# Attention on one core: forget term, scaling and row extreme in one chained VectorE pass

## The chip, the cores and the metric

The kernel runs on one core of a Trainium2 chip. A core has five engines with a queue each: TensorE (PE; its weight loads are shown apart, as PEld), VectorE (DVE), ScalarE (ACT), GpSimd (POOL) and SyncE (SP, which issues DMAs). The metric is the device time of one execution in microseconds, and of several runs the median.

## The reference

One layer of a streaming encoder over 16 meta tokens and 1,024 frames: a norm, then forgetting attention beside a state-space model, merged by gates, an output projection, and a gated feed-forward with a short convolution. The change touches the softmax of the attention alone (8 heads of 64 columns, 1,040 positions):

```python
scale = 1.0 / math.sqrt(dh)          # 0.125
s = jnp.einsum('bqhd,bkhd->bhqk', qb, k, preferred_element_type=jnp.float32) * scale
s = s + jnp.transpose(fqb, (0, 2, 1))[..., None] - fk     # forget term: F[t] - F[s]
mask = k_pos[None, :] <= qp[:, None]
s = jnp.where(mask[None, None], s, -1e30)
p = jax.nn.softmax(s, axis=-1)
return jnp.einsum('bhqk,bkhd->bqhd', p.astype(v.dtype), v)
```

F[t] is the same for a whole row, so it falls out of the softmax.

## The kernel before

All matrix products keep a float32 operand as two parts (high and low) and add three products, lines L170 to L172. The attention goes over four pairs of heads (loop `pr`). In a pair, a unit is one head and one or two row tiles `c` of 128 query rows (the first tile has the 16 meta tokens); `KS[c]` is the number of keys up to the tile's end, `kc`, between 16 and 1,040. `scores` makes the softmax weights of one tile, `pv` multiplies those of a unit with the values, and units are staggered: the scores of a unit are written ahead of the value product of the unit before.

In `scores` (L796 to L833), the keys are cut into banks of up to 512 columns. For each, two matmuls (L817, L818) write raw scores into one of two PSUM buffers `sp`. VectorE then takes them out in pieces (L823): those left of the diagonal with the row of the forget term `fb` (-8 F[s], the same for all 128 partitions), the last one with `fm`, the diagonal block of `fb` with the upper triangle set to -1e30 by GpSimd (L807). Each pass adds the term, writes the sum to `pt` and leaves the maximum of its piece in a column of `mx`; in the profile it is a CUSTOM_DVE instruction and a READ_ACCUMULATOR, which writes the column (in the built order, ISA and ISA again). A tile has one to four pieces (`ns`). L828 takes the maximum of the columns (where there are several) and L829 multiplies it by -0.125. ScalarE computes Exp with that bias, scale 0.125, and the row's sum (L830); L831 inverts the sum on VectorE, and L832 scales the row on GpSimd. There are four `pt` buffers.

In `pv`, TensorE transposes blocks of `pt` into a PSUM buffer `tp` (L860, two buffers), ScalarE casts them to the high part `th` (L867), VectorE computes the low part `tl` (L868, recorded at the helper's line L137), and TensorE multiplies both with the values into `po` (L881, L882). L885 and L886 take the result out.

Beside this, `fill` strews other matmuls between those of the attention: the projection of the next pair's queries and keys and the gates (L170 to L172, three PSUM buffers `mm`). Their results go out through ScalarE (L600 to L610) and VectorE splits (L137).

The order of each engine's queue isn't the order of the code: a scheduler fixes it when the program is built, by its own estimate of what will be ready when. All engines then run their queues strictly in that order. So an edit in `scores` can move instructions of the whole attention.

Of the kernel before, what the change touches and what calls it, by code (L numbers as in the profile page):

```python
# [9 lines left out]
F = mybir.dt.float32  # L10
# [3 lines left out]
AF = mybir.ActivationFunctionType  # L14
ALU = mybir.AluOpType
AX = mybir.AxisListType
# [3 lines left out]
P = 128  # L20
# [38 lines left out]
def block_kernel(ctx, tc, x, meta, xbt, x0t, g1t, w_q, w_k, w_v, w_f, w_u, w_g, b_f, w_ao, lam_d, bw_d, cw_d,  # L59
                 d_sk, l_dt, w_glu, w_o, g2, w_up, cwt_d, w_dn, gf, out, dbg=None, upto=99):  # L60
    nc = tc.nc
    dbg = dbg or {}
    out = out[0]

    V, S, GP, PE, SY = nc.vector, nc.scalar, nc.gpsimd, nc.tensor, nc.sync

    def pool(stack, name, bufs=1, side=None, **k):
        return stack.enter_context(
            tc.tile_pool(name=name, bufs=bufs, side=side, reuse_waits="tile", **k))
# [9 lines left out]
    def mm_ps():  # L79
        mm_n[0] += 1  # L80
        if mm_n[1] and mm_n[0] % 4 == 0:
            return po_ps()
        return pp.tile([P, 512], F, tag="mm", name="mm", bufs=3)
# [4 lines left out]
    def s_ps(name="sp"):  # L88
        return pp.tile([P, 512], F, tag="sp", name=name, bufs=2)
# [304 lines left out]
    def u_product(b, m):  # L394
        ps = mm_ps()
        for k in range(KD):
            part(ps, m, k, *UBLK[b])
        return ps
# [28 lines left out]
    for m in range(4):  # L427
        ps = u_product(1, m)
        S.copy(us_part(1, m), by_chunks(ps[:, :UBLK[1][1]]))
    for b in (2, 3):  # L430
# [15 lines left out]
        for m in range(4):  # L446
            ps = u_product(b, m)
# [341 lines left out]
    ap = pool(st_a, "attn", side="left")  # L789
# [6 lines left out]
    def scores(t_, e, c, fb):  # L796
        t, n = TILES[c]
        kc = KS[c]
        Qs, Ks = t_[f"q{e}"], t_[f"k{e}"]
        hr = slice(64 * e, 64 * e + 64)  # L800
        m_ = max(n, 32)
        dg = kc - n

        qz = qzero[e][c % 2]
        GP.tensor_copy(qz[hr, :m_], Qs[hr, t:t + m_].bitcast(F))
        fm = ap.tile([P, P], F, tag="fm", name="fm", bufs=2)
        GP.affine_select(out=fm[:n, :n], in_=fb[:n, dg:kc], pattern=[[-1, n]],  # L807
                         compare_op=ALU.is_ge, fill=-1e30, base=0, channel_multiplier=1)
        pt = ap.tile([P, L], F, tag="pt", name="pt", bufs=4)
        mx = ap.tile([P, 4], F, tag="mx", name="mx", bufs=4)  # L810
        nb = -(-kc // 512)
        w = -(-kc // nb // 8) * 8
        ns = 0
        for b in range(nb):
            a0, a1 = b * w, min(kc, b * w + w)
            ps = s_ps()
            PE.matmul(ps[:m_, :a1 - a0], Qs[:, t:t + m_], Ks[:, a0:a1], start=True, stop=False)  # L817
            PE.matmul(ps[:m_, :a1 - a0], qz[:, :m_], t_["kl"][:, a0:a1], start=False, stop=True)  # L818
            for lo, hi, src in ((a0, min(a1, dg), fb), (max(a0, dg), a1, None)):
                if hi <= lo:  # L820
                    continue
                s_ = fb[:n, lo:hi] if src is not None else fm[:n, lo - dg:hi - dg]
                V.tensor_tensor_reduce(out=pt[:n, lo:hi], in0=ps[:n, lo - a0:hi - a0], in1=s_, scale=1.0,  # L823
                                       scalar=-3e38, op0=ALU.add, op1=ALU.max, accum_out=mx[:n, ns:ns + 1])
                ns += 1
        nm = ap.tile([P, 4], F, tag="nm", name="nm", bufs=4)
        if ns > 1:
            V.reduce_max(nm[:n, 0:1], mx[:n, :ns], axis=AX.X)  # L828
        V.tensor_scalar(nm[:n, 1:2], nm[:n, 0:1] if ns > 1 else mx[:n, :1], -0.125, None, ALU.mult)  # L829
        S.activation(pt[:n, :kc], pt[:n, :kc], AF.Exp, bias=nm[:n, 1:2], scale=0.125, accum_out=nm[:n, 2:3])  # L830
        V.reciprocal(nm[:n, 3:4], nm[:n, 2:3])  # L831
        GP.tensor_scalar(pt[:n, :kc], pt[:n, :kc], nm[:n, 3:4], 1.0, ALU.mult, ALU.mult)  # L832
        return pt  # L833

    def pv(h, cs, pts, ob):
# [93 lines left out]
    for pr in range(H // 2):  # L929
# [46 lines left out]
        for n_unit, (cs, e) in enumerate(units):  # L976
            if 0 < pr < 3 and n_unit and n_unit % 2 == 0:
                out_weight_sums(4 * (pr - 1) + n_unit // 2 - 1, marks[-1])
            pts = [scores(qk, e, c, fbs[e]) for c in cs]
            if prev:  # L980
                second(*prev)
            prev = (cs, e, pts)
# [86 lines left out]
    for i in range(KD):  # L1069
# [6 lines left out]
        for t, n in QBLK:  # L1076
            ps = mm_ps()
# [962 lines left out]
```

## Time and profile before

| | us |
|---|---|
| median of three runs | 1444.65 (1443.22 to 1447.25) |
| profiled execution, its own time | 1442.12 |
| its span, first to last instruction | 1440.2 |
| granted TensorE clock, share of full speed | 0.998 |

In the lines of the profile, a group is a line of the kernel, its engine and operation, the tiles it writes and reads (out<-in), shapes and count. A timeline's columns are the start (us), the busy time, engine, line, operation and shape; in brackets stands the engine's idle time ahead of it and what ended that. A wait is put as "who <- for whom: us in total, times, longest us".

### The profile page before, as it was taken

How to read it: one execution, taken by the hardware profiler on the slowest of the kernel's cores; microseconds unless marked ns; L12 is line 12 of the kernel's file. 1: busy time of each engine (PE TensorE's matmuls, PEld its weight loads, DVE VectorE, ACT ScalarE, POOL GpSimd, SP SyncE). 2: the span in 40 equal slices, each digit the busy share in tenths (PEclk: the TensorE clock that was granted, in tenths of full speed). 3: DMA queues.
4: the chain of work that ended last, by engine and by line, in shares of the span. 5: the costliest groups of instructions: out<-in, count | busy, mean ns of one | idle time of the engine just before them, and what ended most of it. 6: DMA issues, size and time to landing. Idle time of an engine off the chain costs nothing.

```text
span 1440.2 us, 26617 instructions
## 1 busy us (share of the span) xinstructions
PE 1422.0 (99%) x9655; PEld 1346.8 (94%) x9655; DVE 1069.2 (74%) x2201; ACT 722.9 (50%) x1421; POOL 766.2 (53%) x887
## 2 busy tenths in 40 slices
PE   8999999999999999999999999999999999999997
PEld 8999999988999999999879999999999999888886
DVE  7999788843657676656469987788787875798867
ACT  7646585423646565533646544444443445643443
POOL 1542258642466556515861335455655545788795
PEclk9999999999999999999999999999999999999999
DMA  8686644530147422167963255677744327964443
GB/s 304 169 182 164 152 104 149 151 107 30 38 125 167 125 71 67 45 220 245 265 150 134 72 140 161 165 180 192 185 132 114 95 78 255 329 213 132 127 93 117
DMA packets 92967, 214.05 MB, mean 149 GB/s; under 512 B 15090, under 2 KB 22898, under 8 KB 92452
## 3 DMA queue, kind: packets, MB, share of 16 engines
q1 hardware_dynamic: 74132, 168.15, 35.3%
q0 software_dynamic: 17696, 41.29, 15.1%
q10 hardware_dynamic: 1008, 2.91, 0.5%
q8 instruction: 76, 1.25, 0.4%
q14 instruction: 55, 0.45, 0.1%
HBM read 170.88 MB, written 71.71 MB: 168 GB/s over the span
## 4 chain that ended last, share of the span: by engine, by line
PE 94%; DMA 2%; issue 2%; DVE 1%; ACT 1%; POOL 1%; POOLq 0%; DVEq 0%; SPq 0%; ACTq 0%
PE mm L172 5%; PE mm L170 5%; PE mm L171 5%; PE sp L233 4%; PE sp L232 4%; PE sp L234 4%; PE mm L232 3%; PE mm L234 3%; PE tp L232 3%; PE mm L233 3%; PE tp L233 3%; PE tp L234 3%; PE tp L860 3%; PE mm L1563 2%; PE mm L1562 2%; PE mm L1561 2%
## 5 line engine op out<-in xcount | busy, mean ns | idle before, releaser
L170 PE MATMUL mm<-xhi,whi 128*128 128x342 f32 (+2 forms) x480 | 157.0, 327 | 1.2 <-DVE q L137 1.0
L172 PE MATMUL mm<-xhi,wlo 128*128 128x342 f32 (+2 forms) x480 | 155.5, 325 | 0.0
L171 PE MATMUL mm<-xlo,whi 128*128 128x342 f32 (+2 forms) x480 | 155.2, 324 | 0.0
L1183 POOL TENSOR_TENSOR ov<-ov,og 128x1024 f32<-128x1024 f32 x21 | 50.8, 2421 | 118.1 <-ACT og L1182 115.7
L137 DVE TENSOR_TENSOR sw<-sf,sw 128x512 fp32r<-128x512 f32 x72 | 72.6, 1008 | 44.8 <-ACT sw L1174 43.6
L1174 ACT CAST sw<-sf 128x512 fp32r<-128x512 f32 x72 | 44.9, 624 | 109.7 <-POOL sf L1321 84.4
L170 PEld LDWEIGHTS mm<-xhi,whi 128*128 128x128 f32 x480 | 90.6, 189 | 2.5 <-PE sp L818 0.8
L172 PEld LDWEIGHTS mm<-xhi,wlo 128*128 128x128 f32 x480 | 90.4, 188 | 0.6 <-issue 0.2
L171 PEld LDWEIGHTS mm<-xlo,whi 128*128 128x128 f32 x480 | 90.5, 189 | 0.2
L867 ACT CAST th<-tp 128x256 fp32r<-128x256 f32 (+3 forms) x120 | 56.1, 471 | 62.1 <-PE tp L860 29.8
L137 DVE TENSOR_TENSOR tl<-tp,th 128x256 fp32r<-128x256 f32 (+3 forms) x120 | 65.1, 546 | 25.6 <-ACT th L867 24.1
L1321 POOL TENSOR_TENSOR sf<-raw,sf 128x512 f32<-128x512 f32 x36 | 63.5, 1764 | 38.7 <-DVE sw L137 38.6
L1321 POOL TENSOR_TENSOR sf<-raw 128x512 f32<-128x512 f32 x36 | 48.6, 1351 | 61.3 <-DMA raw<-in_w_up_dram 38.9
L234 PE MATMUL mm<-xhi,sw 128*128 128x258 f32 (+1 forms) x288 | 81.1, 281 | 0.0
L232 PE MATMUL mm<-xhi,sw 128*128 128x258 f32 (+1 forms) x288 | 80.8, 281 | 0.0
L233 PE MATMUL mm<-xlo,sw 128*128 128x258 f32 (+1 forms) x288 | 80.8, 281 | 0.0
L832 POOL TENSOR_SCALAR pt<-pt,nm 128x144 f32<-128x144 f32 (+4 forms) x72 | 52.3, 739 | 49.6 <-DVE nm L831 48.8
L1373 DVE SCALAR_TENSOR_TENSOR ov<-hv,cwt,ov 128x1024 f32<-128x1024 f32 x36 | 68.4, 1900 | 0.4 <-ACT ov L1371 0.4
L1174 ACT CAST sw<-raw 128x512 fp32r<-128x512 f32 x70 | 43.0, 620 | 47.6 <-PE sp L234 23.9
L830 ACT ACTIVATE pt<-pt,nm 128x144 f32<-128x144 f32 (+4 forms) x72 | 52.9, 735 | 26.4 <-DVE nm L829 26.0
L823 DVE CUSTOM_DVE_ANT_0 pt<-sp,fb 128x328 f32<-128x328 f32 (+8 forms) x112 | 46.4, 430 | 20.0 <-PE sp L818 11.0
L137 DVE TENSOR_TENSOR sw<-raw,sw 128x512 fp32r<-128x512 f32 x70 | 57.2, 821 | 5.2 <-ACT sw L1174 4.9
(719 smaller groups left out, 5726.3 us busy)
## 6 DMA issues: line engine op xcount, KB each, us to landing
raw<-in_w_up_dram SPq DMA_DIRECT2D x44, 512.0 KB, 3.7
t_d<-in_w_dn_dram POOLq DMA_DIRECT2D x44, 256.0 KB, 7.1
wr<-t_d SPq DMA_DIRECT2D x44, 256.0 KB, 3.9
ar<-a_d SPq DMA_DIRECT2D x41, 256.0 KB, 5.2
a_d<-ov SPq DMA_DIRECT2D x18, 512.0 KB, 2.6
wr<-in_w_dn_dram SPq DMA_DIRECT2D x33, 256.0 KB, 4.0
t_d<-in_w_dn_dram SPq DMA_DIRECT2D x22, 256.0 KB, 4.5
t_d<-t_d SPq DMA_DIRECT2D x22, 256.0 KB, 4.8
```

Source lines behind the costliest of these rows:

```text
L137: return eng.tensor_tensor(out_, src, hi.bitcast(F), ALU.subtract)
L170: yield PE.matmul(ps, whi[:, i, :], ahi[:, i], start=(i == 0), stop=False)
L171: yield PE.matmul(ps, whi[:, i, :], alo[:, i], start=False, stop=False)
L172: yield PE.matmul(ps, wlo[:, i, :], ahi[:, i], start=False, stop=(i == k - 1))
L232: PE.matmul(ps, a[0][:, i], bh, start=(i == 0 and not joins), stop=False, skip_group_check=True)
L233: PE.matmul(ps, a[0][:, i], bl, start=False, stop=False, skip_group_check=True)
L234: PE.matmul(ps, a[1][:, i], bh, start=False, stop=(i == kh - 1), skip_group_check=True)
L830: S.activation(pt[:n, :kc], pt[:n, :kc], AF.Exp, bias=nm[:n, 1:2], scale=0.125, accum_out=nm[:n, 2:3])
L867: S.copy(th[:kn, z:tw], tp[:kn, z:tw])
L1174: S.copy(hi, src)
L1321: sums.append(GP.tensor_tensor(f_, a, b, op))
L1373: V.scalar_tensor_tensor(out=o, in0=h_[:, j:SEQ + j], scalar=cwc(j, m), in1=o, op0=ALU.mult, op1=ALU.add)
```

## The change

The scale goes into the pass (-0.125 there), so that it leaves negated scores in `pt`, and the extreme becomes a minimum, whose result is the bias of Exp as it stands. In place of a column for each piece that is reduced afterwards, each pass starts its minimum from the column of the pass before (`low`). L828 and L829 fall away, `nm` has two columns and not four, and Exp takes scale -1 and the last column of `mx` as bias.

```diff
+        low = 3e38
         ...
-                V.tensor_tensor_reduce(out=pt[:n, lo:hi], in0=ps[:n, lo - a0:hi - a0], in1=s_, scale=1.0,
-                                       scalar=-3e38, op0=ALU.add, op1=ALU.max, accum_out=mx[:n, ns:ns + 1])
+                V.tensor_tensor_reduce(out=pt[:n, lo:hi], in0=ps[:n, lo - a0:hi - a0], in1=s_, scale=-0.125,
+                                       scalar=low, op0=ALU.add, op1=ALU.min, accum_out=mx[:n, ns:ns + 1])
+                low = mx[:n, ns:ns + 1]
                 ns += 1
-        nm = ap.tile([P, 4], F, tag="nm", name="nm", bufs=4)
-        if ns > 1:
-            V.reduce_max(nm[:n, 0:1], mx[:n, :ns], axis=AX.X)
-        V.tensor_scalar(nm[:n, 1:2], nm[:n, 0:1] if ns > 1 else mx[:n, :1], -0.125, None, ALU.mult)
-        S.activation(pt[:n, :kc], pt[:n, :kc], AF.Exp, bias=nm[:n, 1:2], scale=0.125, accum_out=nm[:n, 2:3])
-        V.reciprocal(nm[:n, 3:4], nm[:n, 2:3])
-        GP.tensor_scalar(pt[:n, :kc], pt[:n, :kc], nm[:n, 3:4], 1.0, ALU.mult, ALU.mult)
+        nm = ap.tile([P, 2], F, tag="nm", name="nm", bufs=4)
+        S.activation(pt[:n, :kc], pt[:n, :kc], AF.Exp, bias=low, scale=-1.0, accum_out=nm[:n, 0:1])
+        V.reciprocal(nm[:n, 1:2], nm[:n, 0:1])
+        GP.tensor_scalar(pt[:n, :kc], pt[:n, :kc], nm[:n, 1:2], 1.0, ALU.mult, ALU.mult)
```

The built order is the same up to the attention and behind it. Within it, VectorE's queue changes most. In the first pair of heads, before, these rows stand on VectorE around the three passes over a tile with 784 keys (`pt_4646`, pieces of 392, 264 and 128):

```order
L823 ISA pt_4646,mx_4647<-sp_4648,fb_4181 128x392
L823 ISA mx_4647 128x1
L831 RECIPROCAL nm_4635<-nm_4635 128x1
L823 ISA pt_4646,mx_4647<-sp_4652,fb_4181 128x264
L823 ISA mx_4647 128x1
L823 ISA pt_4646,mx_4647<-sp_4652,fm_4642 128x128
L823 ISA mx_4647 128x1
L886 TENSOR_TENSOR ob_4537<-po_4538,ot_4616 64x256
L137 TENSOR_TENSOR tl_4677<-tp_4671,th_4676 128x512
L828 TENSOR_REDUCE nm_4657<-mx_4647 128x1
L829 TENSOR_SCALAR nm_4657<-nm_4657 128x1
```

Of the changed kernel, the next tile with such pieces in the same pair (`pt_4751`; lines behind L823 lie a line further down, or a line up behind L828):

```order
L824 ISA pt_4751,mx_4752<-sp_4753,fb_4183 128x392
L824 ISA mx_4752 128x1
L824 ISA pt_4731,mx_4732<-sp_4737,fm_4727,mx_4732 128x128
L824 ISA mx_4732 128x1
L830 RECIPROCAL nm_4742<-nm_4742 128x1
L885 TENSOR_TENSOR ob_4519<-po_4641,ot_4722 64x256
L137 TENSOR_TENSOR tl_4772<-tp_4768,th_4771 128x256
L824 ISA pt_4751,mx_4752<-sp_4757,fb_4183,mx_4752 128x264
L824 ISA mx_4752 128x1
L137 TENSOR_TENSOR tl_4781<-tp_4775,th_4780 128x512
L824 ISA pt_4751,mx_4752<-sp_4757,fm_4747,mx_4752 128x128
L824 ISA mx_4752 128x1
```

The second and third pass read `mx`, the result of the one before, which is the link; the scheduler puts work of other rows between the links, and the two small instructions are gone.

On TensorE, at the first place where a value product meets the next scores, 10 us into the attention, these stood before (`sp_4433` is the second bank of a tile of 528 keys, `po_4352` the first value product of a whole tile):

```order
L860 MATMUL tp_4360<-ident_66,pt_4271 128x128
L860 MATMUL tp_4360<-ident_66,pt_4289 128x128
L817 MATMUL sp_4433<-k0_2519,q0_2517 128x264
L818 MATMUL sp_4433<-kl_2521,qz00_4173 128x264
L881 MATMUL po_4352<-th_4356,vt_3888 128x256
L817 MATMUL sp_4504<-k1_2520,q1_2518 128x400
L818 MATMUL sp_4504<-kl_2521,qz11_4176 128x400
L170 MATMUL mm_4735<-xhi_97,whi_4569 128x384
```

and now:

```order
L859 MATMUL tp_4350<-ident_66,pt_4269 128x128
L859 MATMUL tp_4350<-ident_66,pt_4285 128x128
L880 MATMUL po_4342<-th_4346,vt_3888 128x256
L818 MATMUL sp_4421<-k0_2519,q0_2517 128x264
L819 MATMUL sp_4421<-kl_2521,qz00_4173 128x264
L818 MATMUL sp_4490<-k1_2520,q1_2518 128x400
L819 MATMUL sp_4490<-kl_2521,qz11_4176 128x400
L170 MATMUL mm_4713<-xhi_97,whi_4551 128x384
```

The first value product moved ahead of the score pair. On VectorE, the passes that fill and free the banks at this place stood like this (`sp_4411` and `sp_4429` are the two banks):

```order
L823 ISA pt_4409,mx_4410<-sp_4411,fb_4181 128x272
L823 ISA mx_4410 128x1
L823 ISA pt_4409,mx_4410<-sp_4411,fm_4405 128x128
L823 ISA mx_4410 128x1
L823 ISA pt_4427,mx_4428<-sp_4429,fb_4181 128x264
L823 ISA mx_4428 128x1
L137 TENSOR_TENSOR q0_4185<-mm_4470,q0_4185 64x384
L137 TENSOR_TENSOR q1_4186<-mm_4470,q1_4186 64x384
```

and now (`sp_4401` and `sp_4417`):

```order
L824 ISA pt_4399,mx_4400<-sp_4401,fb_4181 128x272
L824 ISA mx_4400 128x1
L824 ISA pt_4415,mx_4416<-sp_4417,fb_4181 128x264
L824 ISA mx_4416 128x1
L824 ISA pt_4399,mx_4400<-sp_4401,fm_4395,mx_4400 128x128
L824 ISA mx_4400 128x1
L137 TENSOR_TENSOR q0_4185<-mm_4456,q0_4185 64x384
L137 TENSOR_TENSOR q1_4186<-mm_4456,q1_4186 64x384
```

The diagonal pass of the first tile, now a linked one, stands behind the first pass of the second tile; the splits of q stand behind all three, as before.

## The prediction

> **What bounds the kernel now.** I read the first part of the page for shares, then the chain that ended last, then windows over the attention, because a share over the whole span hides stages.
>
> ```profile
> span 1440.2 us, 26617 instructions
> ...
> PE 1422.0 (99%) x9655; PEld 1346.8 (94%) x9655; DVE 1069.2 (74%) x2201; ACT 722.9 (50%) x1421; POOL 766.2 (53%) x887
> ...
> PE 94%; DMA 2%; issue 2%; DVE 1%; ACT 1%; POOL 1%; POOLq 0%; DVEq 0%; SPq 0%; ACTq 0%
> ```
>
> TensorE is busy for 1422.0 of 1440.2 us, and 94% of the chain that ended last is its own work; VectorE holds 1% of it. The edited lines (L823 to L831) run between 347 and 612 us, so the next view is the windows of that stretch (columns: length, then busy time of PE, weight load, DVE, ACT and POOL, granted clock, DMA share, GB/s), and who TensorE waited for in it:
>
> ```profile
> 347.00:390.00 43.00, 41.15 (x272) 38.99 (x271) 27.90 (x136) 26.28 (x68) 24.88 (x58) 1.00 0.11 32
> 390.00:460.00 70.00, 69.61 (x489) 67.92 (x488) 45.94 (x199) 39.07 (x96) 39.11 (x80) 1.00 0.50 137
> 460.00:530.00 70.00, 69.69 (x491) 68.15 (x490) 48.11 (x208) 42.38 (x103) 39.40 (x82) 1.00 0.40 99
> 530.00:612.00 82.00, 81.74 (x582) 80.26 (x580) 52.00 (x228) 46.48 (x109) 47.00 (x87) 1.00 0.19 62
> ```
> ```profile
> PE mm L170 <- DVE q L137: 1.0, 2, 0.5
> PE po L882 <- DVE tl L137: 0.9, 3, 0.3
> PE sp L817 <- DVE mx L823: 0.6, 1, 0.6
> ```
>
> TensorE's idle time is 1.85 + 0.39 + 0.31 + 0.26 = 2.8 us of 265, at a full clock. VectorE is busy for 27.90 + 45.94 + 48.11 + 52.00 = 174 us and so has 91 us free. Of TensorE's named waits only the last (0.6 us, once) is for an edited pass; the split of q queued behind such passes (1.0 us) is the other that the edit can touch.
>
> Busy time can flatter TensorE, as matmul ends are modelled. So I looked at starts, in a quiet and in a disturbed place:
>
> ```profile
> 473.12 0.60 PE L860 MATMUL tp<-ident,pt 128*128 128x128 f32 x4
> 473.47 0.41 PE L170 MATMUL mm<-xhi,whi 128*128 128x342 f32 x1
> 473.71 0.32 PE L171 MATMUL mm<-xlo,whi 128*128 128x342 f32 x1
> 473.87 0.32 PE L172 MATMUL mm<-xhi,wlo 128*128 128x342 f32 x1
> ```
> ```profile
> 419.39 0.38 PE L881 MATMUL po<-th,vt 128*128 128x256 f32 x1
> 420.11 0.38 PE L882 MATMUL po<-tl,vt 128*128 128x256 f32 x1 [0.34 <-DVE tl L137]
> 420.33 0.28 PE L881 MATMUL po<-th,vt 128*128 128x256 f32 x1
> 420.45 0.28 PE L882 MATMUL po<-tl,vt 128*128 128x256 f32 x1
> ```
>
> A 342-column matmul has a slot of 0.16 us until the next starts (473.71 to 473.87); right behind a run of transposes it is 0.24 us (473.47 to 473.71), 0.08 more. At 419.39 a slot that is 0.12 us in the last two rows took 0.72: 0.60 lost, of which the page calls 0.34 idle. So true waiting is up to about twice the idle time: an estimate of 5.6 us for the stage. That is the most that any cure of TensorE's waits here can bring, 0.4%. The Trainium skill, page "Trainium Kernel Development and Optimization", section "Performance Expectations", warns of just this: matmul busy time is a bad measure, and weight-load busy time a good one. The weight-load column above (67.92 of 70.00 us) leaves more room than the matmul column (69.61), 2.08 instead of 0.39 us, which by that rule is a bound on the gain of the same small size.
>
> **What goes.** A row tile's passes stand on VectorE; the small instructions behind them are these:
>
> ```profile
> L828 DVE TENSOR_REDUCE nm<-mx x64: 132/151/158, 350.9 to 609.1; 128x1 f32<-128x3 f32 x32, 128x1 f32<-128x2 f32 x24, 128x1 f32<-128x4 f32 x8
> L829 DVE TENSOR_SCALAR nm<-nm x64: 130/153/157, 351.1 to 609.2; 128x1 f32<-128x1 f32 x64
> L829 DVE TENSOR_SCALAR nm<-mx x8: 135/141/142, 348.1 to 549.0; 16x1 f32<-16x1 f32 x8
> L823 DVE CUSTOM_DVE_ANT_0 pt<-sp,fb x112: 168/436/633, 350.4 to 608.4; 128x264 f32<-128x264 f32 x16, 128x328 f32<-128x328 f32 x16, 128x352 f32<-128x352 f32 x16, 128x16 f32<-128x16 f32 x8
> L823 DVE CUSTOM_DVE_ANT_0 pt<-sp,fm x72: 151/285/292, 347.9 to 608.7; 128x128 f32<-128x128 f32 x64, 16x16 f32<-16x16 f32 x8
> ```
>
> Removed: 64 x 0.151 + 64 x 0.153 + 8 x 0.141 = 9.7 + 9.8 + 1.1 = **20.6 us of VectorE**. The 112 + 72 = 184 passes stay, in the same shapes; another scale, a minimum for a maximum, and Exp with scale -1 and its bias from another tile change no size, so I put them at nothing.
>
> **What comes.** 184 - 72 = 112 passes now read the running extreme of the pass before as a [128, 1] operand, and so wait for its accumulator read. Such a wait is shown at the reduction:
>
> ```profile
> 382.52 0.43 DVE L823 CUSTOM_DVE_ANT_0 pt<-sp,fb 128x264 f32<-128x264 f32 x1
> 382.87 0.08 DVE L823 DVE_READ_ACCUMULATOR2_ANT mx<- 128x1 f32 x1
> 382.87 0.29 DVE L823 CUSTOM_DVE_ANT_0 pt<-sp,fm 128x128 f32<-128x128 f32 x1
> 383.08 0.08 DVE L823 DVE_READ_ACCUMULATOR2_ANT mx<- 128x1 f32 x1
> 383.20 0.15 DVE L828 TENSOR_REDUCE nm<-mx 128x1 f32<-128x3 f32 x1
> 383.39 0.15 DVE L829 TENSOR_SCALAR nm<-nm 128x1 f32<-128x1 f32 x1
> ```
> ```profile
> 383.57 0.95 ACT L830 ACTIVATE pt<-pt,nm 128x784 f32<-128x784 f32 x1 [1.92 <-DVE nm L829]
> ```
>
> A pass that needs nothing of the one before starts together with the accumulator read (382.87 and 382.87); the reduction, which needs it, starts 0.12 us after that read's start (383.08 to 383.20). I price a link at 0.12 us. In the built order 42 of the 112 links stand directly behind their own accumulator read, 42 x 0.12 = 5.0 us; between the ends of the other 70 stands at least one other VectorE instruction, and those cost VectorE nothing (0.12 us each, 8.4 us more, if that cover were gone). The Trainium skill, page "VectorE: DVE Perf Modes", section "The DRAIN you can't avoid", has it that a semaphore between two VectorE instructions costs nothing extra, since the next one waits for the pipeline anyway. The rows above disagree, 0.12 us against 0.00; by that page the 5.0 us would be 0. The per-partition operand itself has no row: its price lies between nothing and a whole small instruction, 0.15 us (L829), or 16.8 us for 112. Below nothing it cannot lie, since the pass goes over the same elements. I take nothing, the nearest rows being L828 and L829, which differ in what they read and not by 0.01 us in what they take. VectorE thus changes by -20.6 + 5.0 = -15.6 us; the bounds are -20.6 and +9.6 (8.4 and 16.8 us more). Either end is small beside its 91 us free, so neither moves the end by itself.
>
> **The chain of one row.** From the start of the last accumulator read to Exp it takes 383.57 - 383.08 = 0.49 us now, and without the two small steps 0.12: 0.37 less. A row of 2, 3 or 4 pieces gives back 0.12, 0.24 or 0.36 in links where nothing stands between. So Exp is ready 0.25 us earlier for 24 rows, 0.13 for 32, and no earlier for 8. Behind it stand Exp, the reciprocal, GpSimd's scaling and only then the transposes, for which TensorE has no wait worth naming in the list above. What is late next is the bank or the split, not the row.
>
> **TensorE's place in it.** Here is the one wait for a pass, and the split behind it:
>
> ```profile
> 357.67 0.60 PE L860 MATMUL tp<-ident,pt 128*128 128x128 f32 x4
> 358.91 0.39 PE L817 MATMUL sp<-k,q 128*128 128x264 f32 x1 [0.65 <-DVE mx L823]
> ...
> 360.51 0.41 PE L170 MATMUL mm<-xhi,whi 128*128 128x384 f32 x1 [0.48 <-DVE q L137]
> ```
> ```profile
> 358.20 0.44 DVE L823 CUSTOM_DVE_ANT_0 pt<-sp,fb 128x272 f32<-128x272 f32 x1 [1.51 <-PE tp L860]
> ...
> 359.24 1.12 DVE L137 TENSOR_TENSOR q<-mm,q 64x384 fp32r<-64x384 f32 x2
> ```
>
> The transposes free a pt buffer, three passes follow, then the two splits until 360.36, and L170 starts at 360.51. In the new order (shown with the change) TensorE puts the value product ahead of the two score pairs here, and VectorE puts the 264-column pass ahead of the diagonal one, so the bank of the first comes free some 0.35 us later (the slot of such a pass, 382.52 to 382.87). TensorE then waits for ScalarE's cast of the transposes instead of the bank, but the same three passes and two splits still end near 360.4, and L170 cannot start before. I cost this place at 0. The transposes of 128 columns stand in 113 runs before and 116 now: 3 x 0.08 = **+0.25 us**. The 0.37 us that a row's end gains may spare one of the short split waits: **-0.3 us**, an estimate, for the three named po waits lie at 0.3 at most. The other engines' moves (GpSimd's masks and scalings by a place or two, SyncE two pairs of loads and stores swapped) are covered by the 2.8 us bound: no transfer is named among TensorE's waits.
>
> **Sum.** +0.25 - 0.3 = -0.05, about 0. The profiled execution took 1442.1 us (1440.2 us of span and 1.9 around it), so 1442.1 again; it lies 2.5 below the median of the runs, 1444.65. Forecast for a median: **1444.5 us**.
>
> **Rivals.**
> - *VectorE sets the pace of the attention after all.* For it: the three waits named are all for VectorE. Against: its 91 us free. The Trainium skill, page "VectorE: DVE Perf Modes", section "Rules for kernel authors", says of chained VectorE operations to minimize their count and not the semaphores, and would so count this change as a gain. The time if all waiting went: 1444.65 - 5.6 = 1439 us. Chance 7%.
> - *The links hold PSUM banks.* A bank of scores is free only when all its pieces are read; a diagonal piece that waits, or stands behind another row's pass, frees it later, and TensorE's next L817 waits in the place of the reduction. It decides wherever TensorE asks for the bank again within that delay. If each of the 64 rows with links stalls TensorE for one link, 64 x 0.12 = 7.7 us, 1452 us. For it: 358.91 is such a wait. Against: it happens once in the stage, for 0.6 us. Chance 6%.
> - *It doesn't do what it says:* the pass with the [128, 1] operand is so slow that VectorE becomes the bound. To use up 91 + 20.6 us, 112 passes would have to cost 1.0 us more each, over twice the 0.436 us of one; the stage then grows from zero at that point, 1455 us with 0.1 us beyond it. Chance 2%.
> - Forecast: 85%.
>
> **Numbers.** A measurement of this kernel can tell about 0.3% from no change, 4.3 us: below 1440.3 is faster, above 1449.0 slower. The forecast's own range is 1444.5 with 2.8 us of idle time either way. The repeated runs spread from 1443.2 to 1447.3, so a median can lie a further 1.5 us off: 1440.2 to 1448.8. The first rival gives faster (7%), the second and third slower (8%), and the forecast spills 1% over each edge: faster 8%, same 83%, slower 9%. The range is 1440.2 to 1448.8, which leaves out the rivals, 15%.
>
> **What would show it.** Right: no L828 or L829 on VectorE, 184 passes of the old durations, a chained pass 0.12 us behind its accumulator read, VectorE's busy time down by 15 to 21 us, and TensorE busy for the same 262 us of the attention. Wrong: waits of L817 for L823's bank in number (second rival), passes over 0.6 us at the old shapes (third), or TensorE's slots behind 419.39 and the like at 0.12 us (first).

## The result: 0.16% slower, and where 2 us went

The changed kernel took 1446.8 us (median of 22 runs, 1442.5 to 1452.6), the kernel before beside it 1444.4 (22 runs): a ratio of 1.0016, interval 1.0009 to 1.0023. That is 2.3 us (1.3 to 3.3) more. It lies inside the 0.3% that the prediction called no change, but the interval leaves 1 out: the sum of about zero was wrong by 2 us. The profiled execution took 1447.3 us. Lines L817 to L825 now stand one lower; from Exp on (L829 now) they stand one higher.

The page of the changed kernel, its first lines and the chain that ended last:

```profile
span 1445.4 us, 26567 instructions
...
PE 1422.4 (98%) x9655; PEld 1345.5 (93%) x9655; DVE 1072.3 (74%) x2065; ACT 721.4 (50%) x1421; POOL 762.1 (53%) x887
...
PE 88%; DMA 3%; issue 3%; DVE 2%; ACT 2%; POOL 1%; SPq 0%; POOLq 0%; DVEq 0%; ACTq 0%
```

TensorE does the same work, but holds 88% of the chain, where it held 94%; transfers and three engines have moved in. The windows (columns as before) say where: the second of the four shown before, and one from 347 to 626 us that holds the end of the attention in both kernels, first of the changed kernel, then of the kernel before:

```profile
390.00:460.00 70.00, 68.53 (x475) 66.04 (x474) 42.67 (x159) 38.32 (x95) 39.43 (x81) 1.00 0.51 137
...
347.00:626.00 279.00, 274.15 (x1903) 266.04 (x1902) 174.24 (x640) 157.93 (x385) 152.38 (x311) 1.00 0.31 85
```
```profile
347.00:626.00 279.00, 275.50 (x1917) 268.01 (x1916) 179.72 (x776) 159.49 (x386) 152.35 (x311) 1.00 0.32 88
```

TensorE is busy for 68.53 of the 70 us, where it was 69.61: most of the loss lies between 390 and 460 us. VectorE's busy time in the attention fell from 179.72 to 174.24 us, by 5.5, not by 15.6. (Its total on the page even rose, from 1069.2 to 1072.3 us; one split behind the attention alone took 5.0 us more, see the last section.) TensorE's named waits in the attention, of the changed kernel:

```profile
PE po L880 <- ACT th L866: 1.5, 3, 1.0
PE po L881 <- DVE tl L137: 0.9, 3, 0.3
PE mm L170 <- DVE q L137: 0.8, 2, 0.5
PE po L880 <- DVE ob L885: 0.8, 1, 0.8
```

The wait for a pass is gone, as forecast. New is the last line, a value product that waits for the addition into `ob`, 0.8 us at once; of the 1.5 us for a cast, 1.0 is the place at 358 us whose change of waits was foreseen.

To measure the attention by itself I take a **stage**, from the start of the first score matmul to the start of the last value product on TensorE. Those are the first and the last start in these two groups, of the kernel before and then of the changed one:

```profile
L817 PE MATMUL sp<-k,q x120: 172/323/457, 291.4 to 607.6; 128*128 128x264 f32 x16, 128*128 128x328 f32 x16, 128*128 128x392 f32 x16, 128*128 128x456 f32 x16
...
L882 PE MATMUL po<-tl,vt x200: 251/282/389, 353.4 to 621.8; 128*128 128x256 f32 x96, 16*128 16x16 f32 x4
```
```profile
L818 PE MATMUL sp<-k,q x120: 170/323/457, 291.6 to 610.0; 128*128 128x264 f32 x16, 128*128 128x328 f32 x16, 128*128 128x392 f32 x16, 128*128 128x456 f32 x16
...
L881 PE MATMUL po<-tl,vt x200: 251/281/386, 353.3 to 624.1; 128*128 128x256 f32 x96, 16*128 16x16 f32 x4
```

With two decimals the stage took 621.76 - 291.43 = 330.33 us before and 624.07 - 291.62 = 332.45 after: **2.12 us** longer. TensorE runs the same number of instructions up to any point, so the n-th starts can be set side by side. From 217 us to the attention the two traces agree to 0.02 us; then two steps appear, **place A** (0.05 to 0.92 between 406 and 414 us) and **place B** (0.86 to 1.82 between 441 and 449 us); the rest of the stage adds up to 0.3.

Behind the stage, both profiles of the changed kernel lose another 2.8 us, 0.7 near 970 us and 2.1 near 1304, in code that the change does not touch. With the stage that would be 4.9 us, and the median is 2.3 longer, 3.3 at most: so not every execution can lose all of it. How many do is open. What follows is about the stage.

**Place A.** GpSimd, SyncE, ScalarE and TensorE of the changed kernel, and then of the kernel before:

```profile
400.41 2.40 POOL L137 TENSOR_TENSOR wlo<-raw,whi 128x1024 fp32r<-128x1024 f32 x1
402.78 1.07 POOL L508 TENSOR_SCALAR gs<-gs 128x1026 f32<-128x1026 f32 x1
402.84 0.33 SPq L148 DMA_DIRECT2D raw<-in_w_g_dram  x1
403.88 0.32 SPq L512 DMA_DIRECT2D g_d<-gs  x1
410.67 0.46 ACT L499 ACTIVATE gs<-mm 128x342 f32<-128x342 f32 x1 [5.63 <-DMA g_d<-gs]
...
411.10 0.32 PE L170 MATMUL mm<-xhi,whi 128*128 128x342 f32 x1
411.65 0.39 PE L880 MATMUL po<-th,vt 128*128 128x256 f32 x1 [0.23 <-ACT th L866]
```
```profile
400.61 1.08 POOL L508 TENSOR_SCALAR gs<-gs 128x1026 f32<-128x1026 f32 x1
...
401.71 0.32 SPq L512 DMA_DIRECT2D g_d<-gs  x1
...
406.47 0.46 ACT L499 ACTIVATE gs<-mm 128x342 f32<-128x342 f32 x1 [1.49 <-DMA g_d<-gs]
```

The scheduler put GpSimd's scaling of a finished gate behind a weight split of 2.40 us. The store of that gate, `g_d`, goes out 2.2 us later, and on SyncE behind a load of 512 KB. `gs` has one buffer, so ScalarE's next gate step waits for the store, now 5.63 instead of 1.49 us, and everything queued behind that step on ScalarE waits too: the cast `th`, for which TensorE leaves a slot of 0.55 us at 411.10 where it takes 0.16.

**Place B.** The same view some 40 us on, of the changed kernel and then of the kernel before:

```profile
439.78 0.74 ACT L829 ACTIVATE pt<-pt,mx 128x528 f32<-128x528 f32 x1 [0.73 <-DVE mx L824]
...
441.10 0.37 ACT L884 COPY ot<-po 64x256 f32<-64x256 f32 x1
...
442.34 0.33 SPq L963 DMA_DIRECT2D o_d<-ob  x1
...
449.07 0.30 PE L859 MATMUL tp<-ident,pt 128*128 128x128 f32 x1
...
449.70 0.42 DVE L885 TENSOR_TENSOR ob<-po,ot 64x256 f32<-64x256 f32 x1 [0.78 <-DMA o_d<-ob]
...
450.17 0.39 PE L880 MATMUL po<-th,vt 128*128 128x256 f32 x1 [0.80 <-DVE ob L885]
```
```profile
438.78 0.37 ACT L885 COPY ot<-po 64x256 f32<-64x256 f32 x1
439.31 0.74 ACT L830 ACTIVATE pt<-pt,nm 128x528 f32<-128x528 f32 x1 [0.16 <-DVE nm L829]
...
440.35 0.33 SPq L964 DMA_DIRECT2D o_d<-ob  x1
...
446.83 0.42 DVE L886 TENSOR_TENSOR ob<-po,ot 64x256 f32<-64x256 f32 x1 [0.55 <-DMA o_d<-ob]
...
447.97 0.28 PE L881 MATMUL po<-th,vt 128*128 128x256 f32 x1
```

Before, ScalarE took the finished value sums out (`ot`) ahead of the Exp of 528 columns; now the Exp stands ahead of the copy, and has to wait for its chained passes. The addition into `ob` and the store of `ob` start later, and this store is slow, because GpSimd's queue is loading `w_o`: the transfers issued from 434 to 443 us in the changed kernel (issues, KB each, median us to landing):

```profile
to_d<-in_w_o_dram POOLq DMA_DIRECT2D x2, 1024.0 KB, 10.6
o_d<-ob SPq DMA_DIRECT2D x1, 128.0 KB, 7.3
```

`ob` has one buffer and `po` one bank, so the next addition waits for the landing, and TensorE for the addition. Before, the addition was done at 447.25, 0.7 us ahead of TensorE's turn at 447.97. The Trainium skill, page "DMA: Bandwidth & Descriptors", section "Issuing engines are not separate DMA queues", says that transfers that ScalarE, SyncE or GpSimd start run on the same DMA engines and interleave there; the rows agree, a store from SyncE of 7.3 us beside two loads from GpSimd. That these loads are what makes it slow is tested below.

### The profile page after: what moved, and what is told of

Same layout as the page of the kernel before. It is cut to its first block, busy times and chain, and to the rows that moved or that the text cites. A ratio compares the mean times of both kernels' runs of the same rounds, so it can differ in the third digit from the quotient of the medians.

```text
span 1445.4 us, 26567 instructions
## 1 busy us (share of the span) xinstructions
PE 1422.4 (98%) x9655; PEld 1345.5 (93%) x9655; DVE 1072.3 (74%) x2065; ACT 721.4 (50%) x1421; POOL 762.1 (53%) x887
## 4 chain that ended last, share of the span: by engine, by line
PE 88%; DMA 3%; issue 3%; DVE 2%; ACT 2%; POOL 1%; SPq 0%; POOLq 0%; DVEq 0%; ACTq 0%
PE mm L170 5%; PE mm L172 5%; PE mm L171 5%; PE sp L232 4%; PE sp L233 4%; PE sp L234 4%; PE tp L233 3%; PE tp L232 3%; PE tp L234 3%; PE mm L234 3%; PE mm L232 3%; PE mm L233 3%; PE tp L859 2%; PE mm L1562 2%; PE mm L1561 2%
## 5 line engine op out<-in xcount | busy, mean ns | idle before, releaser
L137 DVE TENSOR_TENSOR sw<-sf,sw 128x512 fp32r<-128x512 f32 x72 | 78.0, 1083 | 48.1 <-ACT sw L1173 48.0
L829 ACT ACTIVATE pt<-pt,mx 128x144 f32<-128x144 f32 (+4 forms) x72 | 53.0, 736 | 41.7 <-DVE mx L824 41.1
L880 PE MATMUL po<-th,vt 128*128 128x256 f32 (+1 forms) x200 | 57.0, 299 | 2.4 <-ACT th L866 1.5
```

The costliest lines, as they stand in the source:

```text
L137: return eng.tensor_tensor(out_, src, hi.bitcast(F), ALU.subtract)
L880: PE.matmul(po[:, :w], vt[:kn, kk, h, :], th[:kn, gi * w:gi * w + w], start=(kk == 0), stop=False)
```

## The experiments

**Theory 1:** the time lies in the built order, at A and B: a store that was out of TensorE's way now lands too late. **Theory 2:** the chained passes cost it, at many places (the prediction's second rival and its kin). **Theory 3:** what is outside the stage, or all of it, is scatter.

| run | stage, us | step at A, us | step at B, us | ratio to before, 95% |
|---|---|---|---|---|
| before | 330.33 | 0 | 0 | 1 |
| changed | 332.45 | 0.9 | 1.0 | 1.0016 (1.0009 to 1.0023) |
| `after_again`: changed, profiled again | 331.97 | 0.9 | 0.4 | profile only |
| `a_order`: A cured | 331.45 | -0.1 | 1.0 | 1.0011 (1.0001 to 1.0021) |
| `a_out2`: `ot` with two buffers | 331.94 | 0.6 | 0.1 | 1.0014 (1.0005 to 1.0023) |
| `a_both`: A cured, and `ot` | 331.30 | -0.1 | 0.1 | 1.0011 (1.0002 to 1.0019) |
| `a_load`: A and B cured | 330.69 | -0.1 | 0.1 | 1.0002 (0.9993 to 1.0011) |
| `b_swap`: before, with A | 331.49 | 1.0 | 0 | 1.0015 (1.0006 to 1.0024) |
| `b_copy`: before, with B | 331.84 | 0 | 1.2 | profile only |
| `b_mirror`: before, with both | 331.44 | 0.9 | 0.1 | 1.0013 (1.0004 to 1.0023) |
| `b_load`: before, with B's cure | 330.34 | 0 | 0 | 0.9996 (0.9985 to 1.0007) |
| `columns`: changed, no chain | 331.57 | 0 | 0.2 | 1.0019 (1.0008 to 1.0030) |
| `columns_ptr`: the same, with the operand | 333.10 | 0 | 0.9 | profile only |

A step is what TensorE's n-th starts fall behind those of the kernel before, from 406 to 414 us (A) and from 447 to 448 us (B) on that kernel's clock. Each stage and its steps are from one profile. A microsecond of the stage is 0.0007 of the ratio. Every interval holds the share that its stage gives, but is too wide to part the two places; the stages do that.

**Place A undone, and done by itself.** `after(x, y)` keeps `x` behind `y` in the built order and adds no wait. In the changed kernel (`n_w` counts the calls of the weight loader `wchunk`; `scale_of` and `store_of` hold the scaling and the store of the gate whose weights that call loaded):

```diff
+        cut = split_lo(eng or V, lo, raw, hi)
+        if n_w - 2 in scale_of:
+            after(cut, scale_of[n_w - 2])
+        if n_w - 4 in store_of:
+            after(ld, store_of[n_w - 4])
```

> The changed kernel, with two order constraints that make GpSimd take the gate's scaling ahead of one weight split again, and SyncE the store of g_d ahead of one load of w_g: GpSimd and SyncE then run two instructions each in the order of the kernel before at this one place, and nothing else moves on any engine. The stage (start of the first score matmul to start of the last value product on TensorE) took 330.33 us before and 332.45 changed. Theory 1 (the time lies in the built order: this swap costs some 0.9 us behind the store, near 411 us, and a store of o_d some 1.1 near 449): the two gaps of TensorE at 411 and 413 us go, the stage takes 331.5 and the ratio to before falls from 1.0016 to about 1.0010. Theory 2 (the chained passes cost it, at many places): the stage stays at 332.4, ratio 1.0016.

The stage took 331.45 us, 1.00 less, as theory 1 had it. In `b_swap` the split is kept ahead of that one scaling, in the kernel before (`swap_at` is true for one call alone):

```diff
+        if swap_at(n_w):
+            after(scale_of[n_w - 2], cut)
```

> The kernel before, with one constraint that makes GpSimd take the weight split ahead of the gate's scaling near 402 us, so that SyncE's load of w_g goes ahead of the store of g_d: the same two swaps that the change made there, and nothing else moved on any engine. No pass is chained. Theory 1: TensorE gains a gap of 0.5 to 1 us near 411 us that it did not have, the stage takes 330.8 to 331.3 instead of 330.33 us, ratio 1.0004 to 1.0007. Theory 2: stage 330.3, ratio 1.0000.

331.49, 1.16 us more than before, with every pass as it was. ScalarE's wait, of `a_order` and then of `b_swap`:

```profile
404.36 0.32 SPq L521 DMA_DIRECT2D g_d<-gs  x1
...
410.06 0.46 ACT L508 ACTIVATE gs<-mm 128x342 f32<-128x342 f32 x1 [2.19 <-DMA g_d<-gs]
```
```profile
403.86 0.32 SPq L522 DMA_DIRECT2D g_d<-gs  x1
...
410.35 0.46 ACT L509 ACTIVATE gs<-mm 128x342 f32<-128x342 f32 x1 [5.58 <-DMA g_d<-gs]
```

5.63 us became 2.19, and 1.49 became 5.58. Place A is about half of the stage's loss, and it needs no chained pass.

**Place B, first cure.** The sum goes into `ot` in place and is stored from there, so that no addition waits for `ob`:

```diff
-        ot = ap.tile([64, 256], F, tag="ot", name="ot", bufs=1)
+        ot = ap.tile([P, 256], F, tag="ot", name="ot", bufs=2)[:64]
...
+            V.tensor_tensor(ot[:, :w], po[:64, :w], ot[:, :w], ALU.add)
+            SY.dma_start(o_d[64 * h:64 * h + 64, t:t + w], ot[:, :w])
```

> The changed kernel, but a head's value sum is added in place into ot, which has two buffers, and stored for each head by itself; ob with its one buffer is used for the last pair alone. TensorE's order is untouched; SyncE issues 15 stores more. Theory 1: the 1.07 us that TensorE loses at 449 us, where the bank po waits for an addition that waits for ob's store to land, goes; the stage takes 331.4 us instead of 332.45, ratio about 1.0009. Theory 2: the stage stays at 332.4 (the gap there moves elsewhere), ratio 1.0016.

> The changed kernel with both edits: the old order of scaling and split and of store and load at 411 us, and the value sums in ot with two buffers. Theory 1: both losses go, the stage takes 330.3 to 330.6 us as before the change, ratio 1.0000 to 1.0003, with all 112 chained passes still there. Theory 2: 332 us, ratio 1.0014 or more. Theory 3 (what the median shows beside the stage is scatter): the stage recovers and the ratio does not fall.

331.94 and 331.30: 0.5 and 1.15 us less than the changed kernel, where 1.05 and 1.85 to 2.15 were expected. A miss, and the rows of `a_both` say why:

```profile
438.58 0.37 ACT L893 COPY ot<-po 64x256 f32<-64x256 f32 x1 [1.05 <-DMA o_d<-ot]
...
439.54 0.36 PE L889 MATMUL po<-th,vt 128*128 128x256 f32 x1 [0.39 <-DVE ot L895]
```

Each head now stores by itself, and the copy into `ot` waits for a store two back, among the same loads: the wait moved 11 us ahead. So I took away what slows the store instead.

**Place B, second cure.** The second accumulating load of `w_o` is issued one unit later; on GpSimd's queue it moves behind nine other instructions, and no other engine's order changes:

```diff
-                 [(3, o_block(0, 1), True), (1, o_block(1, 1), True)],
-                 [(2, to_d[3], False)], [(2, o_block(1, 1), True)], [(5, to_d[2], False)], [(5, o_block(1, 0), True)]]
+                 [(3, o_block(0, 1), True)],
+                 [(1, o_block(1, 1), True), (2, to_d[3], False)], [(2, o_block(1, 1), True)], [(5, to_d[2], False)], [(5, o_block(1, 0), True)]]
```

> The changed kernel with the constraints of the first run (scaling ahead of the split, store of g_d ahead of the load) and one more edit: the second accumulating load of w_o into to_d (1 MB in all, on GpSimd's queue) is issued one unit later, some 8 us, behind the store of o_d that TensorE waited for at 450.94 us (1135 ns from a transpose to the value product). No other engine's order moves. Theory 1 (what TensorE waits for there is the landing of that store, beside the big loads: issued 444.41, landed 451.51, 7.09 us): the store lands in about 5 us, the slot of 1135 ns falls to about 0.2, and the stage, 331.45 us in the first run, takes 330.4 to 330.7 with all 112 links in place; ratio 1.0001 to 1.0005. Theory 2 (the chained passes): slot and stage stay, 331.4.

Store and addition of `a_load`, and how long that store took to land there:

```profile
439.92 0.33 SPq L972 DMA_DIRECT2D o_d<-ob  x1
...
446.54 0.41 DVE L894 TENSOR_TENSOR ob<-po,ot 64x256 f32<-64x256 f32 x1
```
```profile
o_d<-ob SPq DMA_DIRECT2D x1, 128.0 KB, 3.0
```

The store lands in 3.0 instead of 7.3 us, the addition no longer waits for it, and the stage is 330.69. With all 112 links in place, 0.36 us is left of 2.12, and the ratio is 1.0002. In the control, the kernel before with the same later load, nothing was gained (one transpose moved on TensorE besides), so the move cures what the change had made and is no gain by itself:

> The kernel before with the later issue of the second accumulating load of w_o, nothing else but one transpose moved on TensorE by a few matmuls. It is the control for the run with both cures: if the later load is a gain of its own, it gains here too. Theory 1: no gain, since TensorE did not wait for the store here (0.7 us to spare at 447.97): stage 330.2 to 330.4 us, ratio 1.0000 within 0.0009. If it gains 0.7 us here as well (329.6), the cure showed only that the load disturbs.

330.34 us.

**Place B made in the kernel before:** the Exp ahead of the copy.

```diff
+        ex = S.activation(pt[:n, :kc], pt[:n, :kc], AF.Exp, bias=nm[:n, 1:2], scale=0.125, accum_out=nm[:n, 2:3])
+        if e == 1 and c == 4 and (3, (1, 2)) in copied:
+            after(copied.pop((3, (1, 2))), ex)
...
+        copied[h, cs] = S.copy(ot[:, :w], po[64:, :w])
```

> The kernel before, with one constraint on ScalarE: the Exp of 528 columns near 439.3 us goes ahead of the copy of ot, which the change's order does too at this place (before: cast, cast, copy, Exp). No pass is chained. The copy at 438.78 moves behind the Exp and its accumulator read (439.31 to 440.14), so the addition into ob and its store move from 440.35 to about 441.5 us, and the store lands at 447.9 to 448.8 instead of 446.74; TensorE asked for the bank at 447.97 with 0.7 us to spare. Theory 1: a slot of TensorE near 448 us grows by 0.4 to 1.2 us, and so does the stage: 330.7 to 331.5 instead of 330.33 us. Theory 2: 330.3.

331.84, even more than forecast (a transpose on TensorE and a reciprocal on VectorE moved by a place or two besides): the store took 7.35 us to release the addition (`b_copy`; 444.14 to 451.49):

```profile
444.14 0.33 SPq L968 DMA_DIRECT2D o_d<-ob  x1
...
451.49 0.42 DVE L890 TENSOR_TENSOR ob<-po,ot 64x256 f32<-64x256 f32 x1 [2.30 <-DMA o_d<-ob]
```

Both orders at once did not add up:

> The kernel before with both orders of the change's at once: the weight split ahead of the gate's scaling (and load ahead of store on SyncE), and the Exp of 528 columns ahead of the copy of ot on ScalarE. No pass, reduction or scaling of the row extreme is touched. Theory 1: the two add up, 1.16 from the first and 1.51 from the second run alone: the stage takes 332.7 to 333.1 us instead of 330.33, as long as or longer than the changed kernel's 332.45, and the ratio is 1.0016 to 1.0020. Theory 2: no more than either alone, below 332.

331.44, where 332.7 to 333.1 were expected: A is there (0.9 us), B is not. Here the addition started at 447.56 us and TensorE's turn was at 448.03, so the store landed just in time, though its copy too stood behind the Exp. B is a matter of tenths of a microsecond. The changed kernel profiled again says the same:

> The changed kernel as it is, profiled once more, to see how far the stage repeats. Theory 1 and theory 2: 332.45 us within 0.1, with the gaps at 411 and 449 us where they were. Theory 3 (scatter): it differs by 0.5 us or more.

331.97: place A repeats to 0.01 us (0.91 after it), place B cost 0.43 instead of 0.96, since the store took 6.8 and not 7.3 us. The stage of the changed kernel is thus 1.6 to 2.1 us longer, and theory 3 explains only the half microsecond between the two, as far as the stage goes.

**The chain taken out, and the operand alone.** `columns` has the new pass without the chain:

```diff
-                low = mx[:n, ns:ns + 1]
...
+        if ns > 1:
+            V.tensor_reduce(out=nm[:n, 1:2], in_=mx[:n, :ns], axis=AX.X, op=ALU.min)
+        low = nm[:n, 1:2] if ns > 1 else mx[:n, :1]
```

> The changed kernel without the chain: each pass starts its minimum from the constant and leaves it in a column of its own, and one VectorE reduction takes the minimum of the columns, as before. So 64 reductions of 0.15 us are back and no pass has a [128, 1] operand; the 72 scalings of nm stay away (10.9 us less of VectorE than before). SyncE's order is that of before. Theory 1 (order and two stores): no gap at 411 us; the stage takes 330.0 to 330.7 us, as the scheduler's moves fall, ratio 0.9997 to 1.0004. Theory 2 (the chain costs 2 us): 330.3 or below. Theories agree on it as long as the order makes no new gap. What it tells: the 128x128 pass is 285 ns again without the operand (350 with it), and whether the shorter VectorE work brings anything at all.

> The run without the chain, with a [128, 1] column of a constant tile (the identity's first column, 0 or 1, which bounds the minimum from above; the softmax allows any bias) as the start of every pass's minimum: the operand alone, with no link between passes. If the operand is what lengthens a chained pass, the 128x128 pass takes 350 ns in all 64, 16x16 too about 215 instead of 151, 184 x 0.065 = 12 us of VectorE more; if the length came from the wait for the pass before, 285 ns. Theory 1: the stage stays within 0.5 us of the run without the operand, unless its order holds back a store again. Theory 2: it is 1 to 2 us longer.

Without any link the stage is 331.57 us, only 0.4 to 0.9 less than with all of them, and the ratio of 1.0019 is no lower: my expectation of 330.7 at most was missed. Its order has no A. B's order is there, the Exp at 439.34 us ahead of the copy at 440.67, but costs 0.2 us. From the first score matmul the store of `ob` goes out after 149.8 us here and after 149.9 in `a_order`, which has all links: so the links are not what makes it late. Other slots grew, 0.4 us near 387 us and 0.5 near 583, where TensorE waits for a cast and for a bank (`columns`):

```profile
387.20 0.38 PE L882 MATMUL po<-th,vt 128*128 128x256 f32 x1 [0.19 <-ACT th L868]
...
583.67 0.45 PE L818 MATMUL sp<-k,q 128*128 128x392 f32 x1 [0.19 <-DVE mx L824]
```

I did not take these apart further. The run shows that 7.8 us less of VectorE's busy time (171.88 between 347 and 626 us, where it was 179.72) brings nothing here, and that another order can cost 1 us with no link in it. In `columns_ptr` the stage is 333.10, 1.5 us more than in `columns`; TensorE waits for the store of `ob` again (0.7 us, once), which is about half of it, and whether the rest is the order or the dearer passes is open. What both settle is the price of the operand. The diagonal pass in the changed kernel, in `columns` and in `columns_ptr` (busy us, mean ns):

```profile
L824 DVE CUSTOM_DVE_ANT_0 pt<-sp,fm,mx 128x128 f32<-128x128 f32 x64 | 22.0, 348 | 4.3
```
```profile
L824 DVE CUSTOM_DVE_ANT_0 pt<-sp,fm 128x128 f32<-128x128 f32 x64 | 18.3, 286 | 0.0
```
```profile
L823 DVE CUSTOM_DVE_ANT_0 pt<-sp,fm,ident 128x128 f32<-128x128 f32 x64 | 22.2, 347 | 0.0
```

286 ns without a [128, 1] operand, 347 with one from a constant tile, 348 with the chained one: 0.06 us are the operand's, not the wait's.

## Why the prediction was wrong, point by point

- **The step that failed** is "The other engines' moves (GpSimd's masks and scalings by a place or two, SyncE two pairs of loads and stores swapped) are covered by the 2.8 us bound: no transfer is named among TensorE's waits." The 2.8 us bound what a cure of existing waits can bring; they do not bound what a new wait costs. A transfer that TensorE never waited for had 0.7 us to spare at B, and at A it was a wait of ScalarE, not TensorE, that grew from 1.49 to 5.63 us. A and B cost 1.0 and 0.4 to 1.0 us. A is one of the moves that the step names; B's, the Exp ahead of the copy on ScalarE, it left out altogether. The prediction followed the places where VectorE and TensorE meet, and not `gs` and `ob`, with one buffer each, from a later store to the engine that waits for its landing.
- **The operand**, put at nothing, costs 0.06 us, 112 x 0.061 = 6.8 us of VectorE. It lies inside the bounds given (0 to 0.15).
- **A link** was priced at 0.12 us from the accumulator read's start. It is 0.23, by the changed kernel's rows:

```profile
439.15 0.08 DVE L824 DVE_READ_ACCUMULATOR2_ANT mx<- 128x1 f32 x1
439.38 0.35 DVE L824 CUSTOM_DVE_ANT_0 pt<-sp,fm,mx 128x128 f32<-128x128 f32 x1
```

  439.15 to 439.38. The reduction that served as the model is a short instruction with one input; a pass that takes its start value from the column is not like it, and why it starts later is open.
- **What goes** was over-counted, and with the operand this is why VectorE's busy time fell by 5.5 us and not by 15 to 21. The 136 removed instructions took 20.2 us by their own times, close to the 20.6 forecast, but partly overlapped others on VectorE: for only 13.0 us of that did nothing else run there. Against these 13.0 stand 7.0 us by which the 184 passes grew (67.7 to 74.7 us by their own times), and 13.0 - 7.0 = 6.0 is close to the measured 5.5.
- **That VectorE's time does not move the end** held: `a_load`, with the dearer links, loses at most 0.36 us by them. So the second rival, 7.7 us by links that hold the banks, is refuted in size, and no wait of a score matmul for a pass is in the list of waits. The third rival (a pass dearer by 1.0 us) did not come either.
- **The first rival**, that removing VectorE's work gains, got its test in `columns`: 7.8 us less, and no gain.
- **The weight-load column** was read in one window (2.08 us of room). Over the four windows it leaves 265 - 255.3 = 9.7 us, against 2.8 by the matmul column, so it did not bound the gain at the same small size. No run here tests which of the two is nearer.
- **The place at 358 us**, costed at 0, was right: TensorE's starts behind it differ by 0.09 us. Removed rows, the count of passes and their unchanged size without the operand came as said.
- **The rivals** lacked the case that came: a store that goes out later, behind another order of GpSimd, SyncE or ScalarE. The range, made of idle time and the scatter of medians, held the time all the same, though not for the cause that came.
- **Still open:** the last 0.36 us of `a_load`; the slots of `columns` and the rest of `columns_ptr`; the 2.8 us behind the stage, and how many executions lose them.

## What to carry to other kernels

When a scheduler reorders queues, list every buffer with one copy that a moved transfer or engine step fills or frees, and follow each to the instruction that waits for it: the slack there, not the idle time now seen, says what the move can cost. A wait that shows nothing today may be 0.7 us from showing. To find which of hundreds of moves costs, pin single pairs of instructions, in both directions, and compare the stage itself, not the median.

## What the runs showed of the chip

- A [128, 1] operand as start value lengthens this pass by 0.06 us at every shape (286 to 347 ns at 128 columns), with or without a wait behind it. The link itself takes 0.23 us from the start of the accumulator read to the next pass. The Trainium skill, page "VectorE: DVE Perf Modes", section "The DRAIN you can't avoid", holds a semaphore between VectorE instructions to be free; an unlinked pass starts together with that read, so here it is not.
- One VectorE instruction can wait for several of GpSimd's in a row. At 1304 us, in code that the change does not touch, a split of the changed kernel and the GpSimd instructions beside it:

```profile
1304.30 5.96 DVE L137 TENSOR_TENSOR op<-ar,op 128x512 fp32r<-128x512 f32 x1
1304.67 1.28 POOL L137 TENSOR_TENSOR xlo<-wr,xlo 128x512 fp32r<-128x512 f32 x1
```

  and the same instruction before:

```profile
1301.26 0.92 DVE L137 TENSOR_TENSOR op<-ar,op 128x512 fp32r<-128x512 f32 x1
1301.56 1.76 POOL L137 TENSOR_TENSOR xlo<-wr,xlo 128x512 fp32r<-128x512 f32 x1
```

  In the kernel before the two engines took turns. In the changed kernel four GpSimd instructions ran through, and the split took 5.96 us, for which TensorE lost 2.1. It came in both profiles of the changed kernel, in `a_both` and in `a_load`, and in no other. If every execution of `a_load` had it, its median would be some 2.4 us longer (0.36 and 2.1); the interval allows 1.6 at most. The Trainium skill, page "SBUF — State Buffer", section "Who interferes with whom", has a VectorE instruction with two SBUF inputs contend with a GpSimd one that reads SBUF, over ports that one engine holds at a time, and says that issue order decides who blocks. The rows agree that the two exclude each other, but not that the first to start wins: the split starts at 1304.30, and the GpSimd instruction of 1304.67 still takes its 1.28 us.
